# The second MLP product of a decoder layer: two weight sets per pass at 512 columns, with their chained sums in two fixed pairs of tiles

## The chip, the cores and the metric

One Trainium2 chip; the kernel runs on one of its cores. The time is device microseconds of one execution; medians over several runs are given. A profiled execution is a run of its own, with its own time, and a trace of it gives start, length and releaser of every instruction.

## The reference

One decoder layer, in float32, over 512 tokens of width 2048. The first sub-layer mixes sliding-window attention and a gated delta rule; the change leaves it alone. What matters here is the channel sub-layer:

```python
def squared_relu_mlp(h, w_up, w_down):      # w_up 2048 x 8192, w_down 8192 x 2048
    a = jax.nn.relu(h @ w_up)
    return (a * a) @ w_down

x = layer_norm(DN_ALPHA * x + mixed, ln1_g, ln1_b)
x = layer_norm(DN_ALPHA * x + squared_relu_mlp(x, w_up, w_down), ln2_g, ln2_b)
```

## The kernel before, in words

**Arithmetic.** Every float32 operand is cut into a `hi` part (rounded to float32r, by ACT, L110) and a `lo` part (the rest, by DVE, L111). A product is then three TensorE products: hi·hi, hi·lo and lo·hi (`mul3`, L105 to L107). Both MLP products use Strassen's scheme: a 2 by 2 block product takes 7 products, numbered m = 0 to 6, in place of 8. The operands of the seven are sums of blocks.

**The second product.** The 8192 rows of `w_down` are taken in 8 groups g of 1024, and the 2048 output columns in 4 sets j of 512. One set (g, j) is a 2 by 2 block of tiles of 128 x 1024 numbers (512 KB each): w11, w12, w21, w22. `down` (L1352) runs two sets side by side, j and j+1: for each m, in the order 0, 3, 4, 6, 2, 1, 5 (`ORDER`), 24 matmuls of 256 columns for the one set, then 24 for the other. A call with two sets has 14 such **operands** of 24 matmuls. There are 15 calls with two sets. Then follows set 2 of the last group alone (`LONE`), and the last 512 columns of the last group as a plain product with the LayerNorm and the output.

**Where the weight sums come from.** For a set, only two tiles are held, `kx` (loaded with w11) and `ky` (loaded with w21). Once an operand has been cut from a tile, the tile is turned into the next operand by a DMA: an accumulating DMA on POOL's queue (L186) adds another block of `w_down` to what stands in the tile, or a plain DMA on SP's queue (L188) loads it anew. `kx` carries m = 0, 4, 2, 5 (three adds between them), `ky` carries m = 3, 6, 1 (one plain load, one add). So `kx` stands at every even place of the order and `ky` at every odd place, and an add may start only when both halves of the cut, ACT's and DVE's, have read the tile.

**What sets the order.** `Stream` (L113) hands out loads and cuts ahead of use. A cut writes one of four slots in SBUF, and a slot comes free when TensorE has finished the operand in it, so at most three operands lie ready. Tiles are handed out from lists of free ones: in the second product six tiles tagged `raw` for `kx` and two tagged `T` for `ky`. A recording layer then orders the instructions of each engine; on the chip each engine's queue runs in that order, with waits on semaphores.

**The left operands.** `Rows` (L1287) loads two 1 MB tiles `hf` of the activations of a group and makes the seven cut operands (`slot`) with sums (`st`) on DVE, in seven steps spread over the two calls of the group before.

**Evacuation.** After the 24 matmuls of an operand DVE adds the PSUM bank `b` to the result `y`, which lies in the tile `mix` (L1001), 512 numbers per partition.

Of the kernel before, what the change touches and what calls it, by code (L numbers as in the profile page):

```python
# [42 lines left out]
NT = 2  # L43
# [11 lines left out]
def hymba_layer(ctx: ExitStack, tc: tile.TileContext, i, out, dbg=None):  # L55
# [57 lines left out]
    class Stream:  # L113
# [5 lines left out]

        def __init__(self, pool, raws, cuts):  # L120
            self.loads = {"raw": deque(), "T": deque()}
            self.raw_free = {"raw": deque(), "T": deque()}
            self.live = {"raw": deque(), "T": deque()}
            self.ops, self.ready = deque(), deque()
            self.raws, self.last, self.n_cut, self.n_op = {}, {}, 0, 0
            self.cut_free, self.used = deque(), []
            self.room(pool, raws, cuts)

        def room(self, pool, raws, cuts, tag="raw"):
            self.raw_free[tag].extend([(pool, raws)] * raws)  # L130
            self.cut_free.extend([(pool, cuts)] * cuts)
# [8 lines left out]
        def add(self, keys, make=None, dst=None, then=None):  # L140
            for k in keys:
                self.last[k] = self.n_op
            self.ops.append((self.n_op, keys, make, dst, then))
            self.n_op += 1

        def load(self, tag):
            live, loads, room = self.live[tag], self.loads[tag], self.raw_free[tag]
            while live and self.last[live[0][0]] < self.n_cut:
                room.append(live.popleft()[1])
            if not loads or not room or loads[0][2] > self.n_cut:  # L150
                return False
            key, srcs, _ = loads.popleft()
            a = srcs[0].shape[1]
            pool, bufs = tok = room.popleft()
            raw = pool.tile([P, a, 1024 // a], F32, tag=tag, name=tag, bufs=bufs)
            n = 1024 // a // len(srcs)
            for j, src in enumerate(srcs):
                nc.sync.dma_start(raw[:, :, j * n:(j + 1) * n], src)
# [3 lines left out]

        def cut(self):
            if not self.ops:
                return False
            _, keys, make, dst, then = self.ops[0]
# [4 lines left out]
            src = make(*src) if make else src[0]  # L171
            if callable(dst):
                dst = dst()
            tok = None
            if dst is None:
                pool, bufs = tok = self.cut_free.popleft()
                if bufs:
                    dst = [pool.tile(list(src.shape), F32R, tag=t, name=t, bufs=bufs) for t in ("hi", "lo")]
                else:
                    v = pool.tile([P, 2] + list(src.shape)[1:], F32R, tag="F", name="hl")  # L180
                    dst = v[:, 0], v[:, 1]
            split(*dst, src)
            if then:
                what, nxt_ = then
                if what == "add":
# [7 lines left out]
        def pump(self):  # L193
            while self.load("raw") or self.load("T") or self.cut():
                pass

        def get(self, n=1):

            self.cut_free.extend(t for t in self.used if t)
# [680 lines left out]

    def summed_set(blk, first=False, pool=()):

        t_ = {}

        def plus(name, p, q, out=None):
            if out is None:
                out = tq.tile([P, 4, 256], F32, tag="T", name="T", bufs=NT)
# [37 lines left out]

    def chained_pair(blks, gate=0):
# [3 lines left out]
        for m in ORDER:  # L930
            for (kx, ky), b in zip(keys, blks):
                then = {0: ("add", (0, 1)), 4: ("add", (1, 1)), 2: ("add", (1, 0)),
                        3: ("load", (1, 1)), 6: ("add", (0, 1))}.get(m)
                ws.add([ky if m in (3, 6, 1) else kx], then=then and (then[0], b(*then[1])))

# [31 lines left out]
    tq = ctx.enter_context(tc.tile_pool(name="tq", bufs=NT))  # L967
    ws.room(tq, NT, 0, tag="T")
# [313 lines left out]
    free = deque()  # L1282
# [4 lines left out]
    class Rows:  # L1287
# [8 lines left out]
        def cut(self, m, src):  # L1296
            pool = free.popleft()
            v = op_view(slot(pool))
# [231 lines left out]
```

## Time and profile before

| what | value |
|---|---|
| median of 3 runs | 2233.16 us (2230.01 to 2242.14) |
| the profiled execution | 2244.22 us, span 2242.4 us |
| TensorE busy | 97% of the span |
| second product, two sets per call | about 1578 to 2180 us from the start of the span |

The page names an engine, a line and an operation, then output and input tiles; PE is the matmul, PEld the weight load that runs beside it. A wait is put down to the semaphore that came last. The chain of waits that ended last is read backwards from the last instruction; where TensorE has no idle time, that chain may run through buffers and queues without anything having stood still.

### The profile page before, as it was taken

How to read it: one execution, taken by the hardware profiler on the slowest of the kernel's cores; microseconds unless marked ns; L12 is line 12 of the kernel's file. 1: busy time of each engine (PE TensorE's matmuls, PEld its weight loads, DVE VectorE, ACT ScalarE, POOL GpSimd, SP SyncE). 2: the span in 40 equal slices, each digit the busy share in tenths (PEclk: the TensorE clock that was granted, in tenths of full speed). 3: DMA queues.
4: the chain of work that ended last, by engine and by line, in shares of the span. 5: the costliest groups of instructions: out<-in, count | busy, mean ns of one | idle time of the engine just before them, and what ended most of it. 6: DMA issues, size and time to landing. Idle time of an engine off the chain costs nothing.

```text
span 2242.4 us, 37213 instructions
## 1 busy us (share of the span) xinstructions
PE 2167.1 (97%) x15051; PEld 1986.3 (89%) x15051; DVE 1458.8 (65%) x2170; ACT 982.7 (44%) x1474; POOL 354.1 (16%) x435
## 2 busy tenths in 40 slices
PE   8999999899999999899999999999899999999996
PEld 6777788787888887799999999999899999999995
DVE  4355567565644347867656555668788788778787
ACT  3345325233333224555555555555444444444442
POOL 0122020312110000311121111110111211211113
PEclk9999999999999999899999999999999999999998
DMA  7322332323224231389898898886898888888862
GB/s 206 94 71 71 94 110 65 94 72 82 77 77 169 94 99 62 114 216 231 207 203 214 207 204 213 208 196 212 193 226 213 194 220 210 198 212 215 202 150 94
DMA packets 157480, 352.65 MB, mean 157 GB/s; under 512 B 16539, under 2 KB 84812, under 8 KB 154748
## 3 DMA queue, kind: packets, MB, share of 16 engines
q0 software_dynamic: 40000, 132.46, 32.9%
q1 hardware_dynamic: 117308, 217.82, 28.4%
q8 instruction: 118, 1.93, 0.3%
q14 instruction: 54, 0.44, 0.1%
HBM read 325.01 MB, written 24.66 MB: 156 GB/s over the span
## 4 chain that ended last, share of the span: by engine, by line
PE 71%; issue 12%; DMA 8%; DVE 5%; POOL 2%; ACT 2%; POOLq 0%; SPq 0%; DVEq 0%; ACTq 0%
PE b L107 42%; PE pj L107 16%; PE po L107 8%; DMA raw<-in_w_down_dram 2%; DMA hf<-hd 2%; DMA T<-in_w_down_dram 1%; DVE lo L111 1%; DMA C<-grow 1%; POOL raw L186 1%; DMA tri<-B 1%; PE ps_s L507 1%; PE ps_o L554 1%; DVE mix L1438 1%; PE ps_pt L538 1%; DMA g<-in_ln_dram 1%
## 5 line engine op out<-in xcount | busy, mean ns | idle before, releaser
L107 PE MATMUL b<-slot,hi 128*128 128x256 f32 x3584 | 654.9, 286 | 8.7 <-DVE slot L1040 3.3
L111 DVE TENSOR_TENSOR lo<-raw,hi 128x1024 fp32r<-128x1024 f32 x339 | 417.9, 1233 | 312.1 <-ACT hi L110 311.8
L110 ACT ACTIVATE hi<-raw 128x1024 fp32r<-128x1024 f32 x339 | 358.8, 1059 | 508.5 <-PE b L107 252.5
L107 PEld LDWEIGHTS b<-slot,hi 128*128 128x128 f32 x3584 | 557.6, 191 | 10.6 <-DVE slot L1040 4.1
L107 PE MATMUL b<-slot,lo 128*128 128x256 f32 x1792 | 508.6, 284 | 1.5 <-DVE lo L111 1.5
L107 PE MATMUL b<-hi,slot 128*128 128x256 f32 x2608 | 477.0, 283 | 8.9 <-ACT hi L110 8.9
L107 PE MATMUL pj<-slot,hi 128*128 128x512 f32 x1408 | 462.4, 405 | 0.0
L107 PEld LDWEIGHTS b<-hi,slot 128*128 128x128 f32 x2608 | 406.5, 189 | 9.9 <-ACT hi L110 9.9
L107 PE MATMUL b<-lo,slot 128*128 128x256 f32 x1304 | 368.5, 283 | 0.8 <-DVE lo L111 0.7
L107 PEld LDWEIGHTS b<-slot,lo 128*128 128x128 f32 x1792 | 343.1, 192 | 2.4 <-DVE lo L111 2.4
L107 PEld LDWEIGHTS pj<-slot,hi 128*128 128x128 f32 x1408 | 262.5, 191 | 61.6 <-issue 6.0
L107 PE MATMUL pj<-slot,lo 128*128 128x512 f32 x704 | 283.7, 403 | 6.3 <-DVE lo L111 6.2
L110 ACT ACTIVATE hi<-T 128x1024 fp32r<-128x1024 f32 x164 | 173.7, 1060 | 201.0 <-PE b L107 181.6
L111 DVE TENSOR_TENSOR lo<-T,hi 128x1024 fp32r<-128x1024 f32 x164 | 201.8, 1231 | 83.8 <-ACT hi L110 83.8
L107 PEld LDWEIGHTS b<-lo,slot 128*128 128x128 f32 x1304 | 246.8, 189 | 1.4 <-DVE lo L111 1.3
L1001 DVE TENSOR_TENSOR mix<-mix,b 128x512 f32<-128x512 f32 x223 | 152.8, 686 | 60.6 <-PE b L107 60.2
L107 PE MATMUL b<-hl,slot 128*128 128x256 f32 x1296 | 164.5, 283 | 4.3 <-DVE mix L1001 4.3
L107 PEld LDWEIGHTS pj<-slot,lo 128*128 128x128 f32 x704 | 133.7, 190 | 37.0 <-DVE lo L111 8.3
L107 PEld LDWEIGHTS b<-hl,slot 128*128 128x128 f32 x1296 | 158.8, 191 | 5.7 <-issue 4.1
L186 POOL DMA_DIRECT2D raw<-in_w_down_dram x90 | 77.9, 865 | 496.9 <-DVE lo L111 268.7
L1001 DVE TENSOR_TENSOR F<-F,b 128x512 f32<-128x512 f32 x144 | 99.1, 688 | 82.3 <-PE b L107 80.6
L107 PE MATMUL po<-hi,slot 128*128 128x512 f32 x448 | 141.0, 395 | 0.0
(265 smaller groups left out, 2149.8 us busy)
## 6 DMA issues: line engine op xcount, KB each, us to landing
raw<-in_w_down_dram POOLq DMA_DIRECT2D x90, 512.0 KB, 5.8
raw<-in_w_in_dram SPq DMA_DIRECT2D x88, 512.0 KB, 3.5
raw<-in_w_up_dram POOLq DMA_DIRECT2D x84, 512.0 KB, 6.1
T<-in_w_down_dram SPq DMA_DIRECT2D x60, 512.0 KB, 4.7
T<-in_w_up_dram SPq DMA_DIRECT2D x56, 512.0 KB, 4.9
raw<-in_w_up_dram SPq DMA_DIRECT2D x44, 512.0 KB, 4.3
raw<-in_w_down_dram SPq DMA_DIRECT2D x34, 512.0 KB, 4.5
raw<-in_w_o_dram SPq DMA_DIRECT2D x32, 512.0 KB, 3.6
```

The costliest lines, as they stand in the source:

```text
L107: nc.tensor.matmul(ps, a, b, start=first, stop=last, skip_group_check=more)
L110: nc.scalar.activation(hi, src, AF.Copy)
L111: nc.vector.tensor_tensor(out=lo, in0=src, in1=hi.bitcast(F32), op=ALU.subtract)
L186: nc.gpsimd.dma_start(src, nxt_, accum_op=ALU.add)
L507: nc.tensor.matmul(sc, qT[hp, b * P:(b + 1) * P], kd[hp, e, b * P + k0 - 128:(b + 1) * P], start=True, stop=True)
L538: nc.tensor.transpose(pst[:, (bb * 2 + kk) * P:(bb * 2 + kk + 1) * P], lg[a][:, b, kk * P:(kk + 1) * P], ident)
L554: nc.tensor.matmul(pso[a * 64:(a + 1) * 64, b * P:(b + n) * P], vt[:, b, vf_, vh:vh + 64], pTf[:, (2 * b + 1) * P:(2 * b + 1 + n) * P], st ...
L1001: eng.tensor_tensor(out=dst, in0=p, in1=q, op=op)
L1438: nc.vector.tensor_tensor(out=yt, in0=yt, in1=g, op=ALU.mult)
```

## The change

The second product's calls with two sets no longer alternate between two sets of 256 columns. The two sets lie side by side, and a matmul takes 512 columns, 256 of each. An operand of both sets together would be twice the size, so it is split along the contraction: `kh` = 0 and 1, two k-steps each. A call still has 14 operands; each is now half the contraction of both sets, with 12 matmuls of 512 columns. Token halves t lie in two PSUM banks of their own, and both are evacuated after `kh` = 1.

`chained_wide` takes the place of `chained_pair` for `w_down`. `kx` and `ky` are now pairs of tiles, [128, 2, 1024], of both sets; each cut takes half the contraction out of both members of a pair, and the DMAs for both members are issued after the second half has been cut. Raw tiles, cut slots and temporaries are slices of tiles that are allocated once: `base` with 4 raw tiles (named `raws` in the order), the slots `cuts` (2), `cut3` and `cut4`, one `pair` of 2 tiles, and `kept`, a pair in the place of the tile `F` that held the first product's output. The sums of `Rows` lie in a slot of the pool `sb1`, and one slot is taken from the old `T` tiles instead.

The diff, cut to its core:

```diff
         def load(self, tag):
-            live, loads, room = self.live[tag], self.loads[tag], self.raw_free[tag]
+            live, loads, free = self.live[tag], self.loads[tag], self.free[tag]
             while live and self.last[live[0][0]] < self.n_cut:
-                room.append(live.popleft()[1])
-            if not loads or not room or loads[0][2] > self.n_cut:
+                free.append(live.popleft()[1])
+            if not loads or loads[0][2] > self.n_cut:
+                return False
+            if not free:
+                raw, pairs = self.free["raw"], self.free["W"]
+                if tag == "W" and not self.loads["raw"] and len(raw) == self.n_raw:
+                    raw.clear()
+                    free.extend(self.base[:, j:j + 2, :] for j in range(0, self.n_raw, 2))
+                elif tag == "raw" and not self.loads["W"]:
+                    pair = next((t for t in pairs if t is not self.kept), None)
...
+        def bring(self, raw, srcs, add=False):
+            for n, src in enumerate(srcs):
+                if add:
+                    nc.gpsimd.dma_start(raw[:, n, :], src, accum_op=ALU.add)
+                else:
+                    nc.sync.dma_start(raw[:, n, :], src)
...
+    def chained_wide(blks):
+        def both(i_, j):
+            return tuple(b(i_, j).rearrange("p k c -> p (k c)") for b in blks)
+        kx, ky = ws.block(*both(0, 0), tag="W"), ws.block(*both(1, 0), tag="W")
+        for m in ORDER:
+            for kh in range(2):
+                then = CHAIN.get(m) if kh else None
+                ws.add([ky if m in (3, 6, 1) else kx],
+                       lambda t, kh=kh: t.rearrange("p n (k c) -> p k n c", k=4)[:, 2 * kh:2 * kh + 2],
+                       then=then and (then[0], both(*then[1])))
...
-                chained_pair([down_block(g, j + n) for n in range(2)], gate=ws.n_op if g + j == 0 else 0)
+                chained_wide([down_block(g, j + n) for n in range(2)])
             else:
                 summed_set(down_block(g, j))
...
-            ws.room(p, 2, 0)
-            free.extend([sb1] * 2 + [actp] * 8)
+            ws.room(p.tile([P, 1, 2048], F32R, name="cut4"))
+            ws.free["W"].append(p.tile([P, 2, 1024], F32, name="pair"))
+            free.extend([sb1] + [actp] * 8)
...
+            for kh in range(w):
                 hi, lo = ws.get()
                 for t in range(2):
                     tok = slice(t * P, (t + 1) * P)
-                    for k in range(4):
-                        mul3(ps[:, t * 256:(t + 1) * 256], op[:, 0, k, tok], op[:, 1, k, tok],
-                             hi[:, k, :], lo[:, k, :], first and t == 0 and k == 0, t == 1 and k == 3,
-                             more=not first)
+                    ps, o = (banks[key][t], 0) if w == 2 else (banks[key][0], t * 256)
+                    for k in range(4 // w):
+                        kk = kh * 2 + k
+                        mul3(ps[:, o:o + w * 256], op[:, 0, kk, tok], op[:, 1, kk, tok], hi[:, k, :], lo[:, k, :],
+                             first and kk == 0 and o == 0, kk == 3 and (w == 2 or t == 1), more=not first)
+                    if w == 2 and kh:
+                        for row, col, sign in outs:
+                            v = yj[:, 2 * row + t, :, col * 256:(col + 1) * 256]
+                            sub(nc.vector, v, v, ps.rearrange("p (n c) -> p n c", n=2), ...)
...
-    ws.cut_free.append((fp, 0))
+    F2 = hold["F"].rearrange("p f s -> p (f s)")
+    ws.kept = F2.rearrange("p (n c) -> p n c", n=2)
+    ws.free["W"].append(ws.kept)
```

What the order shows, at three places.

SP's queue before, in one group of the second product. `T` are the `ky` tiles, `raw` the `kx` tiles; the numbers tell one allocation from another.

```order
L158 DMA T_17877<-in_w_down_dram 128x1024
L1292 DMA hf_18090<-hd_7169 128x2048
L158 DMA T_17911<-in_w_down_dram 128x1024
L158 DMA raw_17941<-in_w_down_dram 128x1024
L158 DMA raw_17972<-in_w_down_dram 128x1024
L188 DMA T_17877<-in_w_down_dram 128x1024
L188 DMA T_17911<-in_w_down_dram 128x1024
L158 DMA T_18315<-in_w_down_dram 128x1024
L158 DMA T_18346<-in_w_down_dram 128x1024
L158 DMA raw_18377<-in_w_down_dram 128x1024
L158 DMA raw_18413<-in_w_down_dram 128x1024
```

And SP's queue with the change, from the end of the first product into the second (`raws` are slices of `base`, `F` is `kept`; line 188 is the plain load in `bring`):

```order
L177 DMA raws_87<-in_w_down_dram 128x1024
L1352 DMA hf_13409<-hd_6820 128x2048
L177 DMA raws_87<-in_w_down_dram 128x1024
L1352 DMA hf_13411<-hd_6820 128x2048
L188 DMA pair_13407<-in_w_down_dram 128x1024 x2
L177 DMA raws_87<-in_w_down_dram 128x1024 x2
...
L188 DMA F_7216<-in_w_down_dram 128x1024 x6
L188 DMA pair_13407<-in_w_down_dram 128x1024 x2
L188 DMA F_7216<-in_w_down_dram 128x1024 x2
L1352 DMA hf_14142<-hd_6820 128x2048
L1352 DMA hf_14144<-hd_6820 128x2048
```

From there to the last set every load of a `kx` goes to the one `pair`, two DMAs a call, and every load of a `ky` to `F`. The four `raws` are loaded once at this place and not again before the end of the stage: they hold the four blocks of the last group's lone set, whose loads stand first in the list of the `raw` tag, since the chained pairs have left that list.

DVE's queue before, from the end of one call to the start of the next (L111 cuts, `lo` or `hl` from a raw tile; L1001 evacuates):

```order
L111 TENSOR_TENSOR lo_18374<-raw_17055,hi_18373 128x1024
L1001 TENSOR_TENSOR mix_83<-mix_83,b_18123 128x2x256
L111 TENSOR_TENSOR lo_18410<-raw_17086,hi_18409 128x1024
L1001 TENSOR_TENSOR mix_83<-mix_83,b_18092 128x2x256
L111 TENSOR_TENSOR hl_18440<-raw_17491,hl_18440 128x1024
L1001 TENSOR_TENSOR mix_83<-mix_83,b_18123 128x2x256
L111 TENSOR_TENSOR lo_18470<-raw_17527,hi_18469 128x1024
```

And with the change, at such an end (L110 cuts, L1057 evacuates):

```order
L110 TENSOR_TENSOR cut3_7405<-pair_13407,cut3_7405 128x1024
L1057 TENSOR_TENSOR mix_83<-mix_83,b_15124 128x2x256
L110 TENSOR_TENSOR cuts_88<-pair_13407,cuts_88 128x1024
L1057 TENSOR_TENSOR mix_83<-mix_83,b_15123 128x2x256
L1057 TENSOR_TENSOR mix_83<-mix_83,b_15124 128x2x256
L110 TENSOR_TENSOR cuts_88<-pair_13407,cuts_88 128x1024
L110 TENSOR_TENSOR cut4_13406<-pair_13407,cut4_13406 128x1024
L110 TENSOR_TENSOR cut3_7405<-F_7216,cut3_7405 128x1024
```

Before, the last cuts of a call read raw_17055 and raw_17086, and the first cuts of the next call read two other tiles, raw_17491 and raw_17527. Now the last two cuts and the first two of the next call read the same tile, `pair`; between them stands the load of that tile.

More of the change, by code (lines that the diff above doesn't have):

```diff
@@ L1281, in hymba_layer, with free_slot @@
     fp2s = {}
-    free = deque()
+    free, sums = deque(), []
+    def free_slot():
+        tok = free.popleft()
+        return tok, slot(tok) if tok in (sb1, actp) else tok
     def quads(f0, f1):
```

141 lines of the change are left out of this document (83 added, 58 removed).

## The prediction

> **What bounds the kernel now.** I read the page first, then stretches of the stage, then the chain.
>
> ```profile
> span 2242.4 us, 37213 instructions
> PE 2167.1 (97%) x15051; PEld 1986.3 (89%) x15051; DVE 1458.8 (65%) x2170; ACT 982.7 (44%) x1474; POOL 354.1 (16%) x435
> ...
> 700.00:870.00 170.00, 170.00 (x732) 137.10 (x731) 66.81 (x80) 39.90 (x42) 3.10 (x1) 1.00 0.37 124
> 1565.00:1650.00 85.00, 76.86 (x611) 75.46 (x610) 63.91 (x68) 37.55 (x38) 12.97 (x15) 0.94 0.87 219
> 1578.40:2180.00 601.60, 596.05 (x4972) 594.25 (x4973) 477.85 (x503) 269.18 (x260) 101.27 (x117) 1.00 0.85 204
> ```
>
> The last three rows are busy times by stretch: length, PE, PEld, DVE, ACT, POOL, then granted clock, DMA share and GB/s. TensorE bounds the kernel, and the second product too: in the 601.6 us of its 15 two-set calls it is idle for 5.55 us. That is 601.6 / 15 = 40.1 us per call of 14 operands. The waits of PE there (engine, tile, releaser: us, times, longest) are as small:
>
> ```profile
> PE b L107 <- DVE mix L1001: 4.3, 7, 1.3
> PE b L107 <- ACT hi L110: 1.2, 2, 0.7
> PE b L107 <- DVE lo L111: 0.7, 1, 0.7
> ```
>
> The DMA engines are busy 0.85 of that time, the next highest share. Two rows of the chain (start, length, what) give the pace of both matmul widths without stalls: 512 columns in the output projection, 256 in this stage.
>
> ```profile
> 699.16 173.14 PE po L107 x744
> 1729.46 68.73 PE b L107 x576
> ```
>
> 173.14 / 744 = 232.7 ns and 68.73 / 576 = 119.3 ns. So a call is 336 x 119.3 ns = 40.1 us, as measured, and would be 168 x 232.7 ns = 39.1 us at 512 columns.
>
> **What the wider matmul gains.** 1.0 us a call, 15 us in all, if TensorE stays the bound. The Trainium skill (TensorE: Matmul & The Clock Gate, "Wait — 56ns, not 53.3ns?") has a fixed cost of about 2.5 ns per matmul; halving 5040 matmuls would then be worth 6.3 us, less than the 15 us of the rows.
>
> Evacuations, cuts, sums and DMAs keep number and size; the 4-dimensional access patterns still have runs of 256 numbers. I put them at nothing in busy time. What changes is which of them wait for each other.
>
> **What it costs: one pair for `kx`.** By the order, every `kx` of the stage lives in `pair`. Its life is a loop that nothing overlaps: cut both halves, add, cut, add, cut, add, cut, load the next call's. Before, six raw tiles let the next calls' `kx` stand loaded while this one was still cut, so that only `ky` was reloaded in place, and it has four operands between its last cut and its next use. `kx` has none: place 6 of a call and place 0 of the next are neighbours. If one turn takes longer than TensorE's 39.1 us, TensorE waits for it in every call, whatever lies ready in the three finished slots; slots delay a shortage, they don't pay for one that repeats. So I price one turn.
>
> The cut. The rows are of before, at the start of the stage and in a quiet call (start, length, engine, line):
>
> ```profile
> 1589.12 2.01 ACT L110 ACTIVATE hi<-raw 128x1024 fp32r<-128x1024 f32 x2
> 1827.73 1.06 ACT L110 ACTIVATE hi<-T 128x1024 fp32r<-128x1024 f32 x1 [1.79 <-PE b L107]
> 1828.83 1.23 DVE L111 TENSOR_TENSOR lo<-T,hi 128x1024 fp32r<-128x1024 f32 x1 [0.40 <-ACT hi L110]
> 1588.54 1.22 DVE L111 TENSOR_TENSOR slot<-st,slot 128x1024 fp32r<-128x1024 f32 x1
> 1589.67 1.22 DVE L111 TENSOR_TENSOR hl<-T,hl 128x1024 fp32r<-128x1024 f32 x1
> ```
>
> DVE starts 1.10 us after ACT (1828.83 - 1827.73), a second cut follows 1.13 us later (1589.67 - 1588.54) and takes 1.22: 3.45 us, and 0.1 us from landing to ACT (below), 3.55. Two ACT cuts in 2.01 us don't hold it up.
>
> The adds. Both members of a pair are now added at once. Before has three adds issued as closely as POOL can, with their times to landing, in order:
>
> ```profile
> 1591.18 0.86 POOL L186 DMA_DIRECT2D T<-in_w_down_dram  x1 [5.41 <-DVE hl L111]
> 1592.91 0.86 POOL L186 DMA_DIRECT2D raw<-in_w_down_dram  x1 [0.87 <-DVE lo L111]
> 1594.65 0.86 POOL L186 DMA_DIRECT2D raw<-in_w_down_dram  x1 [0.87 <-DVE lo L111]
> ...
> T<-in_w_down_dram POOLq DMA_DIRECT2D x1, 512.0 KB, 5.2
> raw<-in_w_down_dram POOLq DMA_DIRECT2D x1, 512.0 KB, 6.8
> raw<-in_w_down_dram POOLq DMA_DIRECT2D x1, 512.0 KB, 8.2
> ...
> 1596.47 1.06 ACT L110 ACTIVATE hl<-T 128x1024 fp32r<-128x1024 f32 x1 [5.34 <-DMA T<-in_w_down_dram]
> ```
>
> POOL issues 1.73 us apart and starts 0.29 us after DVE's cut has ended (1591.18 against 1589.67 + 1.22). The landings are 1596.4, 1599.7 and 1602.9: 3.2 to 3.3 us apart, so a pair has landed 1.73 + 6.8 = 8.53 us after its first issue. ACT follows a landing by 0.1 us. An add link is 3.55 + 0.29 + 8.53 = **12.4 us**; TensorE needs four operands, 4 x 12 x 232.7 ns = 11.2 us, for the same two places.
>
> The load, and the speed of both queues over the 645 us from 1565 to 2210 (packets, MB, share of 16 engines):
>
> ```profile
> DMA to landing us min/median/max: 3.6/4.4/5.8
> q0 software_dynamic: 17278, 62.91, 53.9%
> q1 hardware_dynamic: 18203, 63.61, 27.2%
> ```
>
> The first row is the plain load on SP. 27.2% of 645 us for 63.61 MB is 363 GB/s, 1.44 us for 512 KB, so the pair has landed after about 4.4 + 1.44 = 5.8 us. With the same 0.29 us between DVE and the queue, the load link is 3.55 + 0.29 + 5.8 = 9.6 us, against 5.6 us of matmuls in its one place.
>
> One turn: 3 x 12.4 + 9.6 = **46.8 us**. `ky`'s add is issued just behind a `kx` add on the same queue; four adds land by 5.2 + 3 x 3.25 = 15.0 us after the first issue, and the next `kx` add comes 12.4 us after it. It loses (15.0 + 2 x 3.25) - (12.4 + 8.53) = 0.6 us. That is 47.4.
>
> Three things can be added. First, `ky`'s plain load (2 x 1.44 = 2.9 us of all engines) falls into the first `kx` add. Second, `hf`, two loads of 1 MB per two calls, 2.9 us a call. Third, the activations' sums and cuts (1.22 us each in the rows below) now stand in DVE's queue among a pair's two cuts in every other call; three of them in front of the second half are 3.5 us, 1.7 a call on average.
>
> ```profile
> L111 DVE TENSOR_TENSOR slot<-st,slot 128x1024 fp32r<-128x1024 f32 x28 | 34.3, 1224 | 5.7 <-ACT slot L110 5.7
> L1001 DVE TENSOR_TENSOR st<-st,hf 128x1024 f32<-128x1024 f32 x14 | 17.1, 1224 | 0.0
> ...
> 1946.98 0.33 SPq L1292 DMA_DIRECT2D hf<-hd  x1
> 1948.98 0.86 POOL L186 DMA_DIRECT2D T<-in_w_down_dram  x1 [2.00 <-DVE lo L111]
> T<-in_w_down_dram POOLq DMA_DIRECT2D x1, 512.0 KB, 9.3
> 1908.08 0.86 POOL L186 DMA_DIRECT2D T<-in_w_down_dram  x1 [0.87 <-DVE hl L111]
> T<-in_w_down_dram POOLq DMA_DIRECT2D x1, 512.0 KB, 6.9
> ```
>
> The add at 1948.98, 2 us behind an `hf` load, took 9.3 us; the one at 1908.08, in the same place of a call without `hf`, 6.9. So 1 MB of plain load costs an add beside it 2.4 us. I take 2.4 for the first, since it recurs in every turn, and a quarter of the other two, 4.6 us, since they count only where a `kx` transfer or cut is under way just then: 47.4 + 2.4 + 1.1 = **50.9 us a call**. Nothing and all of the three bound a turn between 47.4 and 54.9. The Trainium skill (DMA: Bandwidth & Descriptors, "Queues, rings and completion order") says that each DMA engine goes round-robin between its queues packet by packet; by that rule a plain load takes its full 2.9 us out of an add, the turn would be 51.4 and the time 2397. The trace agrees, with 2.4 of the 2.9.
>
> **The other edits.** `raws`, slots and temporaries as slices: the recorded order of the first product is unchanged up to its last chunk, so nothing. The transition: `ky`'s first load must wait until `F` has been written out; before, the stretch 1565 to 1650 has 8.1 us of idle TensorE at a clock of 0.94. Between 8 us gained (the idle time is absorbed) and 6 us lost (a load of 5.8 us uncovered) I take 0, as the nearest row is a stall of the same kind. The end: the last turn needs no load link but runs out through three add links, a cut and two operands, 3 x 12.4 + 3.55 + 5.6 = 46.4 against 40.1, 6 us. The lone set finds its four blocks loaded: 0.
>
> **Sum**, against the profiled execution's 2244.22 us (span 2242.4): 14 x (50.9 - 40.1) = 151, and 6, is 2401 us. The median of the runs shown, 2233.16, is 0.5% lower than that execution; the same below the sum gives **2390 us**.
>
> **The rivals.**
>
> *TensorE stays the bound* and gains its 15 us: 2244 - 15 = 2229, 2218 by the median. For it: loads land in 4.4 us, PE waits only 6.2 us in the stage, three operands lie ready. Against: take the least of every row. Of the adds between 1890 and 1990 us the fastest landed in 5.1:
>
> ```profile
> DMA to landing us min/median/max: 5.1/6.0/9.4
> ```
>
> An add link is then 3.55 + 0.29 + 1.73 + 5.1 = 10.7 us, the load link, for one member alone, 3.55 + 0.29 + 3.6 = 7.4, and the turn 39.5. Even this floor leaves 0.6 of the 1.0 us. Chance 0.04.
>
> *The turn lies near that floor*, and an evacuation that stands in DVE's queue behind a cut costs TensorE some 0.3 us at each of three neighbouring operands that share a bank, a quarter of the 1.22 of a cut: 15 x 3 x 0.3 = 14 us, which eats the gain. 2233. Chance 0.04.
>
> *The adds land faster than the tight row*, since no third one follows: a turn of 42 to 47, 14 x 2 to 7 and 6 on top, 2267 to 2337 by the median. Chance 0.18.
>
> *Turn 47.4 to 54.9, the forecast*: 2341 to 2445. Chance 0.62.
>
> *Contention feeds on itself*: a late `ky` holds back the cut of `kx` behind it in ACT's queue, and a turn takes 55 to 60; 14 x 15 to 20 and 6 is 216 to 286 on top, 2448 to 2516. For it speaks the 9.4 us to which single adds stretch (last row); against, that the DMA engines have more free time then. Chance 0.12.
>
> **The numbers.** 2285 to 2450 holds the forecast, two thirds of the case below it and the very start of the one above, somewhat under 8 in 10; to reach 8 it goes up to 2455. The forecast's own range is 2341 to 2445. Half a per cent is about what can be told from no change here. Faster 0.04, no change 0.04, slower 0.92.
>
> **What would show it.** In the profile after: PE idle by some 12 us per call in the stage, most of it between the last operands of a call and the first of the next; ACT's cuts from `pair` released by DMAs, not by PE; adds in pairs 1.73 us apart, the second landed about 8.5 us after the first issue; matmuls of this stage at 232 to 233 ns where nothing waits; a lower DMA share than 0.85, 40.1 / 50.9 of it, 0.67; and everything before 1540 us as it was. I am wrong if the stage still takes about 600 us, if cuts from `pair` wait for PE, or if the stretch between calls shows no gap.

## The result, and the profile after

The changed kernel takes 2384.76 us (median of 4 runs, 2382.10 to 2390.17) against 2233.50 for the kernel before on the same chip: 1.0676 of its time, 95% interval 1.0653 to 1.0699. The forecast was 2390. The profiled execution took 2390.17 us, with a span of 2388.4, 146.0 more than before.

The page's head, and busy times by stretch (length, PE, PEld, DVE, ACT, POOL, granted clock, DMA share, GB/s), of the kernel after:

```profile
span 2388.4 us, 32062 instructions
PE 2195.3 (92%) x12531; PEld 1875.3 (79%) x12531; DVE 1450.0 (61%) x2170; ACT 971.7 (41%) x1474; POOL 354.4 (15%) x435
...
0.00:1540.00 1540.00, 1498.15 (x9659) 1326.00 (x9660) 906.74 (x1567) 676.53 (x1169) 227.76 (x302) 0.99 0.54 141
1576.70:2330.00 753.30, 643.31 (x2540) 501.73 (x2541) 465.94 (x501) 260.86 (x261) 101.70 (x116) 0.92 0.67 163
1743.60:1845.60 102.00, 86.92 (x336) 67.62 (x336) 62.88 (x67) 35.09 (x35) 14.04 (x16) 0.90 0.68 165
```

Up to 1540 us the work is the same, and this execution ran it some 8 us ahead of the profiled execution of before. The stage's first load of the activations, `hf`, in SP's timeline of before and of after:

```profile
1536.06 0.33 SPq L1292 DMA_DIRECT2D hf<-hd  x1
```

```profile
1527.86 0.33 SPq L1352 DMA_DIRECT2D hf<-hd  x1
```

The difference lies in the second product: 753.3 us for its 15 calls, where they had 601.6. The last row of the table is two calls: 102 us, in which TensorE works 86.92 and is idle for 15.1, 7.5 a call, at a clock of 0.90.

The pace of two calls can be read from the loads of `hf`, one pair per group of two calls. The first and the last of the six in the middle of the stage, in SP's timeline:

```profile
1631.22 22.32 SPq L1352 DMA_DIRECT2D hf<-hd  x2
...
2140.63 22.01 SPq L1352 DMA_DIRECT2D hf<-hd  x2
```

(2140.63 - 1631.22) / 10 is 50.9 us a call. The same issues before, 40.3 a call:

```profile
1624.78 0.33 SPq L1292 DMA_DIRECT2D hf<-hd  x1
...
2027.49 0.33 SPq L1292 DMA_DIRECT2D hf<-hd  x1
```

All paces below are read in this way.

Who waits for whom, over the 400 us from 1700 to 2100 (engine, tile, releaser: us, times, longest):

```profile
POOL pair L186 <- DVE cut L110: 162.8, 12, 21.5
POOL pair L186 <- DVE cuts L110: 158.7, 11, 22.5
ACT cuts L109 <- DMA pair<-in_w_down_dram: 100.6, 15, 10.2
ACT cut L109 <- DMA pair<-in_w_down_dram: 83.7, 11, 10.5
...
PE b L106 <- DVE mix L1057: 46.7, 18, 5.8
...
ACT cuts L109 <- PE b L106: 17.3, 9, 2.4
...
ACT cut L109 <- PE b L106: 15.1, 9, 3.0
```

The loop is in the rows: POOL waits for DVE's cut, ACT for the pair's DMA, and TensorE behind both. ACT's cuts waited 184.3 us for DMAs of `pair` and 32.4 for TensorE. That TensorE's wait is named after an evacuation (`mix`) is a matter of DVE's queue. PE, DVE and ACT around one such wait:

```profile
1848.61 2.93 PE L106 MATMUL b<-cut,slot 128*128 128x512 f32 x6 [5.65 <-DVE mix L1057]
```

```profile
1846.73 1.22 DVE L110 TENSOR_TENSOR cuts<-pair,cuts 128x1024 fp32r<-128x1024 f32 x1 [6.01 <-ACT cuts L109]
1847.88 0.68 DVE L1057 TENSOR_TENSOR mix<-mix,b 128x512 f32<-128x512 f32 x1
```

```profile
1845.65 1.06 ACT L109 ACTIVATE cuts<-pair 128x1024 fp32r<-128x1024 f32 x1 [8.40 <-DMA pair<-in_w_down_dram]
```

The evacuation stands in DVE's queue behind a cut that waits for ACT, and ACT for the landing of the pair.

Now one turn. ACT's timeline from the first cut after one landing to the same place of the next call, less the rows of `slot` and of `F` that it does not need; then POOL's adds, and SP's load of the next call's pair:

```profile
1817.95 1.06 ACT L109 ACTIVATE cuts<-pair 128x1024 fp32r<-128x1024 f32 x1 [7.30 <-DMA pair<-in_w_down_dram]
...
1829.80 1.06 ACT L109 ACTIVATE cuts<-pair 128x1024 fp32r<-128x1024 f32 x1 [4.63 <-DMA pair<-in_w_down_dram]
1830.76 1.05 ACT L109 ACTIVATE slot<-slot 128x1024 fp32r<-128x1024 f32 x1
1831.71 1.05 ACT L109 ACTIVATE cut<-pair 128x1024 fp32r<-128x1024 f32 x1
...
1859.01 1.06 ACT L109 ACTIVATE cuts<-pair 128x1024 fp32r<-128x1024 f32 x1 [1.66 <-DMA pair<-in_w_down_dram]
...
1869.74 1.06 ACT L109 ACTIVATE cuts<-F 128x1024 fp32r<-128x1024 f32 x1 [2.43 <-PE b L106]
1870.71 1.04 ACT L109 ACTIVATE cut<-pair 128x1024 fp32r<-128x1024 f32 x1
...
1919.44 1.06 ACT L109 ACTIVATE cuts<-pair 128x1024 fp32r<-128x1024 f32 x1 [7.31 <-DMA pair<-in_w_down_dram]
```

```profile
1821.79 1.75 POOL L186 DMA_DIRECT2D pair<-in_w_down_dram  x2 [21.52 <-DVE cut L110]
1834.69 1.75 POOL L186 DMA_DIRECT2D pair<-in_w_down_dram  x2 [11.14 <-DVE cut L110]
...
1851.12 1.75 POOL L186 DMA_DIRECT2D pair<-in_w_down_dram  x2 [8.95 <-DVE cut L110]
```

```profile
1863.24 0.80 SPq L188 DMA_DIRECT2D pair<-in_w_down_dram  x2
```

From ACT's cut to the next issue and from there to ACT's next cut: 3.84 + 8.01, 4.89 + 10.96, 5.47 + 7.89, and for the load 4.23 + 7.47. That is 52.8 us; the call behind it, with no work on the activations, takes 1919.44 - 1870.71 = 48.7. Together 101.5 for two, and no step of one overlaps another. This is the turn that the prediction priced.

### The profile page after: what moved, and what is told of

Its sections match the earlier page's. It is cut to its first block, busy times and chain, and to the rows that moved or that the text cites. A ratio compares the mean times of both kernels' runs of the same rounds, so it can differ in the third digit from the quotient of the medians.

```text
span 2388.4 us, 32062 instructions
## 1 busy us (share of the span) xinstructions
PE 2195.3 (92%) x12531; PEld 1875.3 (79%) x12531; DVE 1450.0 (61%) x2170; ACT 971.7 (41%) x1474; POOL 354.4 (15%) x435
## 4 chain that ended last, share of the span: by engine, by line
PE 56%; DMA 17%; issue 11%; DVE 9%; ACT 3%; POOL 3%; SPq 0%; ACTq 0%; POOLq 0%; DVEq 0%
PE b L106 30%; PE pj L106 14%; DMA pair<-in_w_down_dram 13%; PE po L106 7%; DVE cuts L110 3%; DVE cut L110 2%; ACT cuts L109 1%; POOL pair L186 1%; ACT cut L109 1%; DMA C<-grow 1%; DVE mix L1057 1%; DVE slot L1096 1%; DMA tri<-B 1%; DMA hf<-hd 1%; PE ps_s L540 1%
## 5 line engine op out<-in xcount | busy, mean ns | idle before, releaser
L106 PE MATMUL pj<-slot,cuts 128*128 128x512 f32 x2112 | 533.3, 402 | 6.8 <-DVE cuts L110 6.7
L106 PEld LDWEIGHTS pj<-slot,cuts 128*128 128x128 f32 x2112 | 389.3, 189 | 97.8 <-DVE cuts L110 9.0
L106 PE MATMUL b<-slot,cuts 128*128 128x256 f32 x3672 | 459.0, 285 | 7.1 <-DVE slot L1096 3.2
L106 PEld LDWEIGHTS b<-slot,cuts 128*128 128x128 f32 x3672 | 449.2, 191 | 9.4 <-DVE slot L1096 4.3
L106 PE MATMUL b<-cut,slot 128*128 128x512 f32 (+1 forms) x1356 | 350.7, 411 | 78.1 <-DVE mix L1057 54.0
L110 DVE TENSOR_TENSOR cuts<-raws,cuts 128x1024 fp32r<-128x1024 f32 x204 | 252.5, 1238 | 263.2 <-ACT cuts L109 262.7
L106 PE MATMUL b<-cuts,slot 128*128 128x512 f32 (+1 forms) x1332 | 338.6, 407 | 51.8 <-DVE mix L1057 30.8
L106 PEld LDWEIGHTS b<-cut,slot 128*128 128x128 f32 x1356 | 263.4, 202 | 152.0 <-DVE mix L1057 47.0
L106 PEld LDWEIGHTS b<-cuts,slot 128*128 128x128 f32 x1332 | 258.0, 199 | 121.6 <-issue 20.1
L106 PE MATMUL b<-slot,cut 128*128 128x256 f32 x1704 | 216.5, 283 | 3.4 <-DVE F L1057 3.1
L1057 DVE TENSOR_TENSOR mix<-mix,b 128x512 f32<-128x512 f32 x223 | 149.3, 682 | 106.1 <-PE b L106 105.4
L1057 DVE TENSOR_TENSOR F<-F,b 128x512 f32<-128x512 f32 x144 | 98.9, 687 | 79.7 <-PE b L106 78.3
L110 DVE TENSOR_TENSOR cut<-pair,cut 128x1024 fp32r<-128x1024 f32 x60 | 73.2, 1221 | 82.7 <-ACT cut L109 82.6
L110 DVE TENSOR_TENSOR cuts<-pair,cuts 128x1024 fp32r<-128x1024 f32 x60 | 73.2, 1221 | 69.2 <-ACT cuts L109 69.2
```

Source lines behind the costliest of these rows:

```text
L106: nc.tensor.matmul(ps, a, b, start=first, stop=last, skip_group_check=more)
L110: nc.vector.tensor_tensor(out=lo, in0=src, in1=hi.bitcast(F32), op=ALU.subtract)
L1057: eng.tensor_tensor(out=dst, in0=p, in1=q, op=op)
```

## The experiments

Three questions: does the one pair set the pace, and what part of its turn; is TensorE really outside that turn; and which edit, alone, brings the loss. The edits are against the changed kernel unless it says otherwise. Paces are in us per call. Each ratio is to runs of the kernel before on the same chip as that kernel.

| kernel | us (range) | ratio to before, 95% | pace | PE busy in 1700 to 2100 | clock there |
|---|---|---|---|---|---|
| before | 2233.50 (2230.01 to 2242.14) | | 40.3 | 397.3 | 1.00 |
| after | 2384.76 (2382.10 to 2390.17) | 1.0653 to 1.0699 | 50.9 | 338.8 | 0.91 |
| 256 columns | 2414.42 (2409.64 to 2415.28) | 1.0792 to 1.0824 | 52.6 | 335.0 | 0.90 |
| one pair, fifth slot | 2374.34 (2370.26 to 2375.55) | 1.0605 to 1.0641 | 48.6 | 350.9 | 0.92 |
| two pairs each | 2348.28 (2341.74 to 2350.28) | 1.0502 to 1.0537 | 47.7 | 350.1 | 0.95 |
| two pairs, evacuations first | 2342.93 (2338.17 to 2348.64) | 1.0442 to 1.0504 | 47.7 | 350.5 | 0.94 |
| two pairs, own banks | 2336.46 (2334.98 to 2339.66) | 1.0429 to 1.0465 | 47.2 | 356.9 | 0.96 |
| two pairs, fifth slot | 2296.32 (2288.24 to 2308.66) | 1.0232 to 1.0283 | 44.7 | 366.3 | 0.96 |
| one add of two (2 runs) | 2296.09 (2295.52 to 2296.66) | 1.0240 to 1.0289 | 44.1 | 374.4 | 0.96 |
| adds by halves, one pair | 2304.69 (2300.12 to 2307.75) | 1.0303 to 1.0336 | 44.5 | 372.9 | 0.96 |
| halves and two pairs | 2244.66 (2243.10 to 2250.47) | 1.0040 to 1.0074 | 40.3 | 391.4 | 1.00 |
| ... and evacuations first | 2250.36 (2240.78 to 2258.79) | 1.0022 to 1.0073 | 40.6 | 389.6 | 0.99 |
| ... and a fifth slot | 2250.54 (2240.41 to 2261.20) | 1.0039 to 1.0090 | 41.1 | 383.6 | 0.99 |
| before, `kx` in tiles of its own | 2244.88 (2239.74 to 2251.53) | 1.0028 to 1.0059 | 40.8 | 392.8 | 1.00 |

**Two narrow matmuls for each wide one.** If TensorE waits in every call, more TensorE work costs nothing.

```diff
+                        for q in range(w):
+                            cs = slice(q * 256, (q + 1) * 256)
-                            mul3(ps[:, o:o + w * 256], ..., hi[:, k, :], lo[:, k, :], ...)
+                            mul3(ps[:, o + q * 256:o + (q + 1) * 256], ..., hi[:, k, cs], lo[:, k, cs], ...)
```

> The changed kernel with each 512-column matmul of the two-set calls made as two of 256 columns; tiles, cuts, DMAs and banks as changed. Theory (loop): TensorE's work per call grows from 39.1 to 40.1 us and stays below the turn of 51 us, so no change: 2375 to 2400 us. Rival A (the wide pass itself costs): back towards before, 2240 to 2320.

It took 30 us more, against no change expected: 1.7 a call, the 1.0 us of extra matmul time and some. So TensorE's work is not free, although in the changed kernel TensorE is idle for 7.5 us a call: somewhere it stands in the loop. ACT's cuts waited for TensorE for 76.4 us from 1700 to 2100, against 32.4. It also says that the wide matmul is a gain in this kernel.

**A second pair for each operand.** The four raw tiles become two more pairs, so that four pairs are taken in turn, and the lone set's blocks, which held them, load late.

```diff
-                if tag == "W" and not self.loads["raw"] and len(raw) == self.n_raw:
+                if tag == "W" and not (self.loads["raw"] and self.loads["raw"][0][2] <= self.n_cut) and len(raw) == self.n_raw:
...
-                summed_set(down_block(g, j))
+                summed_set(down_block(g, j), gate=ws.n_op - 4)
```

> The changed kernel, but the four raw tiles are not filled with the last lone set's blocks at the start of the stage; they serve as two more pairs, so a call's kx and ky stand in other pairs than the last call's. Same adds, loads, cuts, matmuls. Theory (the loop through the one pair of kx sets the time): the load link of 9 to 11 us leaves the loop; what is left is three add links of 12.4 to 13.4 us, and the next call's first cut follows the last one after 2 us: a turn of 41 to 45 us in place of 51, 14 x 6 to 10 = 84 to 140 us less, 2245 to 2300 us. Rival A (what costs is the pass itself: 512 columns with two banks, and evacuations behind cuts): no change, 2375 to 2395. Rival B (what costs is that two adds are issued at once and share the DMA engines, and TensorE's lower clock after gaps): little change, above 2340.

A miss: the pace fell by 3.2, not by the load link's 9.6. Between a call's last landing and the next call's first add there are still 11.5 and 11.2 us, against 16.0 and 13.1 in the changed kernel. ACT's timeline at such a place, and its waits from 1700 to 2100, of this kernel:

```profile
1783.06 1.06 ACT L109 ACTIVATE cut<-pair 128x1024 fp32r<-128x1024 f32 x1 [2.62 <-DMA pair<-in_w_down_dram]
...
1789.17 1.06 ACT L109 ACTIVATE cuts<-raws 128x1024 fp32r<-128x1024 f32 x1 [3.61 <-PE b L106]
1791.94 1.06 ACT L109 ACTIVATE cut<-raws 128x1024 fp32r<-128x1024 f32 x1 [1.71 <-PE b L106]
```

```profile
ACT cuts L109 <- PE b L106: 64.2, 26, 5.6
ACT cuts L109 <- DMA raws<-in_w_down_dram: 62.8, 12, 10.7
ACT cut L109 <- PE b L106: 58.9, 34, 3.0
ACT cut L109 <- DMA pair<-in_w_down_dram: 39.5, 11, 7.1
```

The next call's data is there, but its first two cuts wait for slots that TensorE still reads. ACT now waits 123 us for TensorE and 102 for the pairs' DMAs. The wait on the load had become a wait on slots.

**Two pairs, evacuations first.** A rival for what is left: a waiting cut holds back an evacuation, and with it TensorE.

```diff
-                hi, lo = ws.get()
+                hi, lo = ws.get(late=w == 2 and kh == 1)
...
+            if w == 2:
+                ws.pump()
```

(`late` leaves out the two calls of `pump` in `get`, so that the next cut is issued behind the operand's evacuations.)

> As e1_two_pairs_each, with the cut that used to be issued between an operand's two halves issued after the evacuations of that operand, so that in DVE's queue no evacuation stands behind a cut that waits for a DMA. Theory now (in e1 the chain goes on through TensorE: a late cut holds the evacuation behind it in DVE's queue, TensorE waits for that bank although operands lie ready, and the slots it then frees late hold back the next call's first cut): TensorE's 61 us of waits for evacuations go, a call falls from 48.5 to 42 to 45 us, 2250 to 2300 us. Rival (the three add links alone, longer than I priced them, set 48.5 us): 2335 to 2355.

Nothing moved in the pace, but the edit did not bring what it was made for. TensorE still waited 37.2 us for evacuations from 1700 to 2100, against 35.7 without the edit, up to 6.39 us at a time. DVE's timeline of this kernel, just ahead of that wait's end at 1825.96:

```profile
1824.08 1.23 DVE L110 TENSOR_TENSOR cuts<-raws,cuts 128x1024 fp32r<-128x1024 f32 x1 [6.28 <-ACT cuts L109]
1825.22 0.68 DVE L1059 TENSOR_TENSOR mix<-mix,b 128x512 f32<-128x512 f32 x1
```

An evacuation still stands behind a waiting cut, so this run leaves the rival open. The next one settles it.

**Two pairs, each product in banks of its own.** The sums of products that share a bank are left out, so that no operand waits for a bank of its neighbour.

```diff
+            key = m if w == 2 else key
```

> As e1_two_pairs_each, with two PSUM banks of its own for each of the seven products of a two-set call; it leaves out the sums that neighbouring products build up in a shared bank, each product is evacuated alone, with the same number of evacuations. Theory (evacuations behind waiting cuts hold TensorE by the shared bank): TensorE no longer waits for the evacuation of the operand just before, 2250 to 2310 us. Rival (add links alone): 2335 to 2355.

Here TensorE no longer waits for evacuations: from 1700 to 2100 it waits 43.0 us for cuts and none for `mix`. The pace hardly moved (47.2). So evacuations behind waiting cuts are a trace of the loop, not a cause of it. The adds of two calls here landed 8.9 us after their first issue on average, a landing was followed by the next issue after 4.3 to 6.1, and the boundary took 8.4 and 10.1: the links set the pace, not the banks.

**Two pairs and a fifth slot.** The last pool's `pair` gives its place to a slot; the two pairs are the first product's raw tiles. With `F` that makes three pairs, which both operands take in turn, where the kernel with four slots had four.

```diff
-            ws.room(p.tile([P, 1, 2048], F32R, name="cut4"))
-            ws.free["W"].append(p.tile([P, 2, 1024], F32, name="pair"))
+            ws.room(p.tile([P, 2, 2048], F32R, name="cut4"))
```

> Two pairs for each operand, with a fifth slot for finished cuts in the place of the pair that came from the last pool; the four raw tiles of the first product are the two pairs, and the first load waits until they are empty. With the four slots, 11.5 us passed between a call's last landing and the next call's first add, since the next call's first cuts waited 3.6 and 1.7 us for slots that TensorE still read. If the slots set that, it falls by 3 to 5 us a call: 14 x 3 to 5 is 42 to 70 us less than 2348, and up to 8 us for the later first load: 2278 to 2315 us. If the adds' links alone set the pace, with the boundary only filled by waiting, 2335 to 2360 us.

The first `hf` of the first and of the last couple of loads, ten calls apart:

```profile
1624.41 0.33 SPq L1352 DMA_DIRECT2D hf<-hd  x1
...
2071.72 0.33 SPq L1352 DMA_DIRECT2D hf<-hd  x1
```

The pace fell by 3.0, to 44.7, and the time by 52 us, as the theory of the slots said, and that with one pair fewer. TensorE's reading had stood in the turn through the slots.

**One pair and a fifth slot.** The test of a sentence of the prediction, that slots delay a shortage and don't pay for one that repeats.

```diff
-                    raw.clear()
-                    free.extend(self.base[:, j:j + 2, :] for j in range(0, self.n_raw, 2))
+                    raw = self.free["raw"] = deque(self.base[:, j, :] for j in (2, 3))
+                    free.append(self.base[:, 0:2, :])
...
-            ws.room(p.tile([P, 1, 2048], F32R, name="cut4"))
-            ws.free["W"].append(p.tile([P, 2, 1024], F32, name="pair"))
+            ws.room(p.tile([P, 2, 2048], F32R, name="cut4"))
```

(The edit of the lone set's gate is also in this kernel and in the one before.)

> The changed kernel with a fifth slot for finished cuts: kx's one pair is two of the first product's raw tiles, the pair of the last pool gives its place to the slot, and the lone set's blocks load late into the other two raw tiles. The prediction held that slots delay a shortage and don't pay for one that repeats: then one turn of the pair still sets the pace, and the time stays at 2370 to 2400 us. Rival: with four slots TensorE's reading is a part of the turn, as the run with 256 columns and the fifth slot beside two pairs (52 us) suggest; then the fifth slot takes 2 to 4 us out of each call here too: 2385 less 28 to 56, 2325 to 2360 us.

The time, 2374, is in the range of the prediction's rule (2370 to 2400), but the pace says otherwise: 48.6, 2.3 less than with four slots, which is the rival's 2 to 4. The first and the last `hf` of its series, in SP's timeline:

```profile
1642.39 0.33 SPq L1352 DMA_DIRECT2D hf<-hd  x1
...
2128.54 0.33 SPq L1352 DMA_DIRECT2D hf<-hd  x1
```

The series starts 11 us later than the changed kernel's and ends 12 us earlier, so that half of what the ten calls gained had been lost ahead of them. What held up the transition is open: with two pairs, whose first load waits for the same raw tiles, the first `hf` came at 1624.41. A fifth slot is worth 2.3 with one pair and 3.0 with two; more pairs are worth 3.2 with four slots and 3.9 with five. Both together don't take the turn down to TensorE's 39.1.

**One add of two.** The second member's adds are left out, and with them its sums.

```diff
-                    nc.gpsimd.dma_start(raw[:, n, :], src, accum_op=ALU.add)
+                    if n == 0:
+                        nc.gpsimd.dma_start(raw[:, n, :], src, accum_op=ALU.add)
```

> The changed kernel without the adds of the second member of each pair (its sums are left out). Loop through one pair: an add link falls by the 3.3 us of the second add to 9 to 10 us, the turn to 3 x 9 to 10 and a load link of 10, 37 to 41 us: TensorE nearly bounds the stage, 2215 to 2270 us. If the load link or the evacuations held the stage by themselves, it would stay above 2320.

89 us less, 6.8 a call, or 2.3 for each of three links, and 26 us short of the expected range. The median add now landed 5.4 us after its issue, where two had taken 9.0 on average. By these numbers a link should lose 3.6; over a third of that went elsewhere in the turn.

**Adds by halves.** Each half of a pair is added to right behind its own cut, in transfers of 256 KB, and `kx` keeps its one pair.

```diff
-                    self.bring(self.raws[keys[0]], nxt_, add=what == "add")
+                    hs = slice(nxt_[0] * 512, (nxt_[0] + 1) * 512)
+                    self.bring(self.raws[keys[0]][:, :, hs], [s[:, hs] for s in nxt_[1:]], add=what == "add")
...
-                then = CHAIN.get(m) if kh else None
+                then = CHAIN.get(m)
...
-                       then=then and (then[0], both(*then[1])))
+                       then=then and (then[0], (kh, *both(*then[1]))))
```

> The changed kernel with one pair for kx as it is, but each chained DMA is issued for half the contraction, right behind the cut of that half: twice as many DMAs of 256 KB. Theory (loop): each half has a loop of its own; a link is one cut 2.4, 0.3 to POOL, and two adds of half the size, 1.73 + 3.6 to 5 us, together 8 to 9.5 us; with a load link of 7 to 10 the turn is 31 to 38 us, below TensorE's 39.1, so TensorE bounds the stage again: 2215 to 2260 us. Rival B (DMA engines and POOL's queue): more and smaller DMAs make it slower or leave it, 2380 or more. Rival A: no change, 2375 to 2395.

80 us less, with the same bytes in twice the transfers: 6.4 a call, or 2.1 for each link. This is the largest effect of one edit that leaves the sums whole, though the expectation was too good by 45 us. What is left of the turn shows when the second pair is added to it (below): 4.2 a call, the load link and what stands around it.

**The kernel before with `kx` in two tiles of its own.** One part of the change alone: no second set of tiles for `kx`, but matmuls of 256 columns, members apart, and each chained DMA behind its own cut.

```diff
-        keys = [(ws.block(b(0, 0)), ws.block(b(1, 0), tag="T", gate=gate)) for b in blks]
+        keys = [(ws.block(b(0, 0), tag=tag), ws.block(b(1, 0), tag="T", gate=gate)) for b in blks]
...
-            ws.room(p, 2, 0)
+            ws.room(p, 2, 0, tag="K")
```

(`tag` is "K" for the two-set calls; the other raw tiles are left to the remaining lone sets.)

> The kernel before, with kx of the second product held in two raw tiles of their own instead of six, so that each is loaded anew only when its last cut is done; the four other raw tiles hold the last lone set's blocks, as in the changed kernel. All chained DMAs stay one per cut. Theory (loop): the loop of one tile is 3 x (2.4 + 0.3 + 5.2 to 6.8) and a load link of 7, 31 to 35 us, below 40.1: no change, 2225 to 2243 us. Rival (holding kx in one buffer costs, whatever its DMAs): 2270 or more.

It costs 10 us, 0.6 a call (40.85 against 40.27), 2 us more than the expected range allows. So the loss of the second set of tiles, which the prediction put first, is not enough by itself. POOL's adds to `kx` in one call of this kernel:

```profile
1886.92 0.86 POOL L184 DMA_DIRECT2D K<-in_w_down_dram  x1 [16.30 <-DVE lo L111]
1888.65 0.86 POOL L184 DMA_DIRECT2D K<-in_w_down_dram  x1 [0.87 <-DVE lo L111]
1896.12 0.86 POOL L184 DMA_DIRECT2D K<-in_w_down_dram  x1 [6.61 <-DVE lo L111]
1899.70 0.86 POOL L184 DMA_DIRECT2D K<-in_w_down_dram  x1 [2.72 <-DVE lo L111]
```

Each member turns for itself: its add is issued behind its own cut and it waits for no second landing. From one add to the next of the same member are 9.2 and 11.1 us, with TensorE's own pace in them; the pairs' were 12.9 and 16.4 (1821.79, 1834.69, 1851.12).

**Halves and two pairs.** Both repairs.

> Both edits: two more pairs, and chained DMAs by halves. Theory (loop): nothing of the chain is left on the path; TensorE at 39.1 us a call, 15 us under before: 2210 to 2235 us. Rival A (wide pass costs by itself): above 2250. Rival B: above 2250 too, with TensorE's waits on cuts released by DMAs.

The loss is gone but for half a per cent; the expected gain over before, 2210 to 2235 us, did not come. ACT's waits and PE's, from 1700 to 2100, of this kernel:

```profile
ACT cuts L109 <- PE b L106: 83.6, 48, 2.3
ACT cut L109 <- PE b L106: 65.3, 39, 2.8
...
ACT cut L109 <- DMA raws<-in_w_down_dram: 7.5, 9, 1.5
ACT cuts L109 <- DMA raws<-in_w_down_dram: 6.9, 5, 1.8
```

```profile
PE b L106 <- DVE mix L1058: 8.6, 10, 1.9
```

The table of waits has turned over: cuts wait 149 us for TensorE and 27 for DMAs, 14 of them for the raw pairs and the rest for `F` and the old pair. TensorE sets the pace again, at 40.3, with 8.6 us of waits for evacuations in ten calls. That is 0.9 a call and eats most of the 1.0 us that the wide matmul gains. Of what is left against before, 2.8 us stand between the stage's first `hf` load (here at 1529.91) and the first `hf` of the ten calls, and 4.2 behind the last; the medians differ by 12.6, so the rest is not located.

**And evacuations first**, where TensorE sets the pace:

> The halves' adds and the second pairs together, with one edit more: the cut that follows the second half of an operand is issued after that operand's evacuations, not ahead of them. With both repairs TensorE sets the pace of the stage again, and its largest wait there is for evacuations (DVE's mix rows, 16.9 us in 15 waits of about 1.1 us). If these waits come from evacuations that stand behind a cut that itself waits, they go: 2222 to 2240 us. If they come from the evacuations' own length, nothing moves: 2240 to 2252 us. In the variant with second pairs alone this edit moved nothing, but there TensorE did not set the pace.

No gain: its waits for `mix` over the stage are 17.9 us, and were 16.9, so here too the edit did not take away what it was made for. **And a fifth slot as well:**

> Halves' adds, second pairs, evacuations first, and the fifth slot. If TensorE already sets the pace with four slots, the fifth changes nothing in the calls and the later first load costs up to 8 us: 2225 to 2250 us. If cuts still wait for slots there, 2215 to 2230 us.

No gain either, with three pairs as in the other kernel with two pairs and a fifth slot; with its waits for evacuations at 4.3 us, TensorE waits 21.3 for the activations' operands, which now come late. No kernel here beats the one before.

## Why the prediction was right, point by point

**The turn.** 50.9 a call forecast, 50.9 measured, and two calls taken apart confirm the structure: three add links and one load link, one after the other. The parts, mean of two calls, against their terms:

- ACT's cut to the next issue, 3.45 + 0.29 = 3.74 forecast: 3.84, and 3.74 and 3.75 in the second call, where nothing else is in DVE's queue; 4.34 on average. The difference, 0.6 a link and 1.8 a call, is mostly the third addition of the prediction, `slot` cuts between a pair's two cuts (the row at 1830.76, and its like), where a quarter of 1.7 was taken; a cut of `F` and an evacuation have a part in it.
- Issue to ACT's next cut, 8.53 + 0.1 = 8.63 forecast: 9.07, from 7.9 to 10.96. The transfers beside it were put at 0.6 + 2.4 + 0.7 = 3.7 a call and cost 3 x 0.44 = 1.3.
- Load link, 9.6 forecast: 10.5. In the call shown the pair's first cut stood in ACT's queue behind one of `F` that waited for TensorE (1869.74).

46.8 plus 4.1 was forecast, 46.8 plus 4.0 came. That the additions agree in sum is partly luck: the one for contention was too large and the ones for queues too small.

**The sum.** 157 us over the profiled execution was forecast (14 x 10.8 and 6), 146 came. But the profiled execution of before had come to the stage 8.2 us later, in work that both kernels share (1536.06 against 1527.86). Counted from there, the difference is 154.2: 14.6 ahead of the first `hf` of the ten calls, 106.7 in the ten calls, where 108 were forecast, and 32.9 behind. The five other calls with the transition and the end thus cost 47.5 us, where 49 were forecast. By the medians the difference is 151.3.

**"TensorE waits for it whatever lies ready in the finished slots."** Half right. With four slots TensorE's reading is part of the turn: 256 columns cost 1.7 a call, and a fifth slot takes off 2.3. But the turn stays far above 39.1 with it. The prediction had put this part of the turn at nothing, so that some of the agreement at 50.9 is luck too.

**Idle time.** About 12 us a call was forecast, most of it between calls. It is 7.5, since TensorE worked slower: 86.9 us for two calls that are 78.2 at 232.7 ns. Three rows of PE show that the full pace was still there where nothing waited:

```profile
1821.11 5.75 PE L106 MATMUL b<-cuts,slot 128*128 128x512 f32 x24
1826.70 5.70 PE L106 MATMUL b<-cut,slot 128*128 128x512 f32 x24
1832.23 5.76 PE L106 MATMUL b<-cuts,slot 128*128 128x512 f32 x24
```

(1832.23 - 1821.11) / 48 is 231.7 ns, as good as the 232 to 233 forecast; over the two calls the mean clock is 0.90. Nor did the idle time lie between calls: the 5.65 us at 1848.61 follow the landing of a call's second add. One sign that the prediction gave for being wrong thus came true: the stretch between two calls shows no gap. TensorE runs without a stop from 1814.34 to 1842.96 and from 1848.61 to 1883.20, and the next call's first cut of `pair` (1817.95 and 1870.71) lies inside both stretches. The operands that lie ready carry TensorE over the load link, and what the turn lacks shows behind the adds.

**The cause.** The prediction named one thing, that `kx` has one pair. The runs show that it takes two: one pair alone costs 10 us in the kernel before. Members that move together, with both adds issued behind the second half's cut and both landings awaited, are the other. The adds by halves, and both repairs together, bear that out for the two halves of a pair; 512 columns with the two members of a pair apart were not run. The prediction had this in its terms (1.73 + 6.8 for a pair, where single adds take 5.1 to 6), but gave the one pair as the reason. Taking either away gave less than its price: 3.2 for the load link of 9.6, since the wait went over to the slots, and 2.1 for each add link, with the load link left in the turn.

**The other signs.** Adds in pairs 1.73 us apart: wrong, POOL issues two in 1.75 us, with their starts mostly 0.5 to 0.7 apart. In the rows that the prediction took for POOL's closest, the second and third adds had each waited 0.87 us for a cut of their own. The second add landed no earlier for it: 7.8 to 10.8 us after the first issue in the two calls shown, where 8.5 were forecast. DMA share 0.67: 0.67. Cuts of `pair` released by DMAs: 184 us, against 32 for TensorE over all of ACT's cuts. Before 1540 us: the same work. Of the rivals, TensorE as the bound is out by the 338.8 of 400 us; faster adds (42 to 47) are what the halves and the one add of two made, not the change; a turn near the floor and one of 55 to 60 are out by the 50.9. (By its own terms that last rival ends at 2518, not 2516.)

## What to carry to other kernels

When a tile is refilled in place, price the loop through it, cut, issue, landing, cut again, against the time in which the consumer eats what one turn delivers; the shares of the engines say nothing of it. A link that waits for two joined transfers is as long as the slower of both: here 9.0 us on average from the first issue to the second landing, where one add alone took 5.4. Issuing each part behind its own cut was the larger repair, 80 of the 151 us. Price a repair by what is late next: removing the 9.6 us load link gave 3.2, because the cut slots stood behind it.

## What the runs showed of the hardware

TensorE's clock fell though TensorE was busy 85% of the time. From 1700 to 2100 us it was 0.90 to 0.92 in kernels that leave TensorE idle for 12 to 16%, 0.94 to 0.96 at 6 to 13%, and 0.99 or 1.00 at 1 to 4%. The share of idle time alone does not give the clock: 12.3% went with 0.92 and 12.5% with 0.95. In the changed kernel the granted clock was 1.00 from 1821.0 to 1837.8 us, where nothing waited, and 0.50 from 1811.6 to 1814.4 and from 1848.6 to 1851.5, behind gaps of 3.52 and 5.65 us. The Trainium skill (TensorE: Matmul & The Clock Gate, "HAM oscillation — how this bites in real kernels") asks for no gaps above some 3.4 us, and shows a clock that is throttled again, to half, behind longer ones. The trace agrees on the half, but not on that length: the clock was also 0.50 from 1885.6 to 1892.0, behind gaps of 2.43 and 0.46 us, and from 1913.0 to 1916.0, behind gaps of 1.83 and 2.67. The prediction did not price the clock, and how much of the loss the idle time hides was not measured.

Two adds of 512 KB on one queue landed within 7.8 to 10.8 us of the first issue in the two calls above, one alone within 5.1 to 8.6 (median 5.4). The second landed 2.6 to 4.8 us behind the first, around the 3.2 to 3.3 us between landings in the kernel before.
